# Two conditioning vectors move from TensorE to VectorE rows, a third one's rows move behind the second norm, and the norms get bf16 fillers

## The chip, the core and the metric

The kernel runs on one core of one Trainium2 chip. The metric is the device time of one execution in microseconds (us), as the median of several runs. A core has a matrix engine (TensorE, in the rows PE, with its weight loads as PEld), a vector engine (VectorE, DVE), an engine for functions of one operand (ScalarE, ACT), GpSimd (POOL), SyncE (SP), whose queue issues the DMAs of this kernel, and 16 DMA engines.

## What is computed

Two layers of a decoder trunk on 256 tokens of 1024 channels, all in fp32. In each layer a token mixer (two attentions and a gated 31-tap convolution, weighted by three sigmoid gates) and a channel mixer (up to 2 x 2816 channels, a 3-tap causal convolution, silu(a) * b, down again) are added to `x`. Both are fed by an RMS norm that is scaled and shifted by vectors computed from the condition `c`, and both are multiplied by a gate vector before they are added:

```python
for l in range(2):
    mod = silu(c) @ w_mod[l] + b_mod[l]                      # 6 x 1024 numbers
    sh1, sc1, g1, sh2, sc2, g2 = split(mod, 6)               # parts 0..5
    h = rms_norm(x, mix_norm_g[l]) * (1 + sc1) + sh1
    x = x + g1 * token_mixer(h, ...)
    h = rms_norm(x, ffn_norm_g[l]) * (1 + sc2) + sh2
    x = x + g2 * channel_mixer(h, ...)
```

`(l, r)` is part `r` of layer `l` in what follows: (0,5) is g2 of layer 0, (1,3) is sh2 of layer 1, (1,2) is g1 of layer 1, (1,4) is sc2 of layer 1.

## The kernel before

**Tiles.** `x` lies transposed: 8 tiles of 128 channels by 256 tokens. Every fp32 product is made of three matmuls on pairs of reduced-precision parts (high by high L316, low by high L317, high by low L319; `flush(whole)` in L310 to L312 keeps the three together). A weight unit (mostly 128x1024, 512 KB) is fetched by SP into one of four `raw` buffers; ScalarE rounds it to `whi` (L232), VectorE subtracts to get `wlo` (L233). `take()` keeps two or three split units ahead of the matmuls. The units come in one fixed list, so every engine's order follows from the program's order and from `tc.issue_after`, which holds an instruction behind another one. Instructions on one engine run strictly in that order.

**The conditioning vectors** are computed in two ways. `mod_part(l, r)` does one on TensorE: 8 loads of 512 KB from `wm`, 32 fp32 matmuls (L424), an ACT copy, two transposes (L432), one VectorE addition (L434). `mod_row(l, r, k)` does an eighth of one on VectorE: a load of 512 KB from `wmr`, one multiply-and-accumulate of 128x1024 (L407) against a row `crow`, one small addition (L408). Eight rows make a vector.

**Where they stand.** (0,5) is a `mod_part` that fills the norm ahead of channel mixer 0: two of its eight steps ahead of the sums, six behind, with the transposes after the second up block. (1,3) is a `mod_part` in the same way in the norm ahead of layer 1. Rows of (1,0) and (1,1) run in channel mixer 0, one per up block. The 8 rows of (1,2) are written one behind each `conv_in(k)` at layer 1's start, but nothing holds them there, and they stand among channel mixer 0's instructions on VectorE. They use four spare buffers (`SPARE`). Rows of (1,4) are spread by tokens `r0` to `r1` over the second half of layer 1's token mixer, whose order is the hand-written list `STEPS[1]`: `G` gates, `O` output projections of the attentions, `LS`/`LB` the norm of the convolution, `OC` its projection, `PR` the last projection. The depthwise convolution on VectorE (L1142) runs from `GLU` (L960) to the mean (L1154) ahead of that norm.

**The norm** (`norm_stats`) is a chain: last matmul, residual into `x` (L1290 or L1462), square on ACT, sums on VectorE (L554) and TensorE (L559), rstd on VectorE and POOL (L536, L537), broadcast by two transposes (L569), then tiles `norm_tile` (L615, ACT, L617). Bf16 matmuls that compute nothing (`warm`, L339, "fillers" here) stand in its gaps: `WARM1 = (4, 7, 3)`. Then layer 1 goes on with `conv_in` (L316 into `psa`, halves `conv_in(0)` to `conv_in(7)`), with `latents(k)` (`KL`) behind it.

## Time and profile before

| what | before |
|---|---|
| median of 3 runs | 898.74 us (898.46 to 899.44) |
| the profiled execution: time, and its span | 905.0 us, 902.9 us |
| busy in the span: PE, DVE, ACT, POOL | 881.3, 807.8, 556.9, 50.7 us |
| norm ahead of channel mixer 0: last matmul before, first after | starts 277.74, 285.35 us |
| norm ahead of layer 1: last matmul before, first after | starts 468.15, 476.19 us |
| mean DMA rate | 222 GB/s |

The profiled execution is one run, 6.3 us longer than the median, with 2.1 us of it outside the span. "Busy" of an engine that has work queued behind its own order says little on whether it sets the end: at each stage one has to look which engine's idle time is zero and who waits for whom. Starts in a row are us from the span's start.

### The profile page before, as it was taken

Reading aid. Unit: us, or ns where it says so; the run is one execution under the profiler, and the core shown is the slowest. Engines: PE = TensorE matmul, PEld = TensorE weight load, DVE = VectorE, ACT = ScalarE, POOL = GpSimd, SP = SyncE. Lnnn points to the kernel's source line nnn. Section 1 sums busy time; section 2 is a strip of 40 time slices with the busy share of each in tenths; the row PEclk is TensorE's granted clock in tenths of the full one; section 3 lists DMA queues with packets and bytes.
Section 4 is the critical chain, followed back from the end, with each engine's and each line's share of the span. In section 5 each row is a group of like instructions: output and inputs, shape, how many; then the busy total and the mean of one; then the engine's idle time right before and its main releaser. Section 6 shows DMA issues by size and latency. Waiting matters only on the chain.

```text
span 902.9 us, 18611 instructions
## 1 busy us (share of the span) xinstructions
PE 881.3 (98%) x7247; PEld 836.2 (93%) x7247; DVE 807.8 (89%) x1592; ACT 556.9 (62%) x998; POOL 50.7 (6%) x36
## 2 busy tenths in 40 slices
PE   8999899999999999999999999999999999999998
PEld 6888788998997999999999988989999999999998
DVE  6989899999988999999875999999987899998774
ACT  4677579744666655556543676788465777556551
POOL 1010710000000000000000034000000000000000
PEclk8999999999999999999999999999999999999999
DMA  8956615598998989997752656157866575987631
GB/s 320 376 202 198 196 59 176 183 318 304 318 315 283 332 273 326 301 318 236 214 176 76 202 184 209 53 164 232 264 205 211 163 232 176 308 281 211 194 95 48
DMA packets 57976, 201.59 MB, mean 223 GB/s; under 512 B 6944, under 2 KB 8480, under 8 KB 57888
## 3 DMA queue, kind: packets, MB, share of 16 engines
q1 hardware_dynamic: 57888, 200.41, 66.9%
q8 instruction: 57, 0.93, 0.4%
q14 instruction: 31, 0.25, 0.1%
HBM read 199.33 MB, written 1.05 MB: 222 GB/s over the span
## 4 chain that ended last, share of the span: by engine, by line
PE 76%; DVE 13%; ACT 4%; DMA 4%; issue 2%; SPq 0%; POOL 0%; DVEq 0%; ACTq 0%; POOLq 0%
PE psb L316 15%; PE psb L317 15%; PE psb L319 15%; PE psa L316 7%; PE psa L317 7%; PE psa L319 7%; DVE wlo L233 4%; DVE cacc L1142 2%; ACT whi L232 2%; DVE raw L817 1%; PE psa L424 1%; PE psa L735 1%; PE psa L747 1%; PE psa L680 1%; DMA raw<-in_win 1%
## 5 line engine op out<-in xcount | busy, mean ns | idle before, releaser
L232 ACT ACTIVATE whi<-raw 128x1024 fp32r<-128x1024 f32 (+2 forms) x286 | 295.4, 1041 | 173.7 <-PE psb L317 90.7
L233 DVE TENSOR_TENSOR wlo<-raw,whi 128x1024 fp32r<-128x1024 f32 (+2 forms) x286 | 340.0, 1194 | 48.2 <-ACT whi L232 40.5
L316 PE MATMUL psb<-hh,whi 128*128 128x256 f32 x1056 | 254.7, 282 | 0.6 <-ACT p L714 0.3
L317 PE MATMUL psb<-hl,whi 128*128 128x256 f32 x1056 | 252.3, 279 | 0.0
L316 PEld LDWEIGHTS psb<-hh,whi 128*128 128x128 f32 x1056 | 198.6, 188 | 5.5 <-issue 3.3
L317 PEld LDWEIGHTS psb<-hl,whi 128*128 128x128 f32 x1056 | 198.8, 188 | 0.5 <-DVE wlo L233 0.4
L319 PE MATMUL psb<-hh,wlo 128*128 128x256 f32 x1056 | 144.2, 278 | 0.0
L319 PEld LDWEIGHTS psb<-hh,wlo 128*128 128x128 f32 x1056 | 131.0, 188 | 0.8 <-issue 0.8
L1142 DVE SCALAR_TENSOR_TENSOR cacc<-upad,cw,cacc 128x256 f32<-128x256 f32 x240 | 105.9, 479 | 0.4
L316 PE MATMUL psa<-mhl,whi 128*128 128x256 f32 x400 | 93.3, 277 | 0.0
L317 PE MATMUL psa<-mhl,whi 128*128 128x256 f32 x400 | 93.1, 276 | 0.0
L537 POOL TENSOR_TENSOR rs<-rs,mhalf 128x8 f32<-128x8 f32 (+3 forms) x26 | 49.1, 1900 | 674.4 <-DVE rs L536 674.4
L1424 DVE SCALAR_TENSOR_TENSOR e<-psb,fw,e 128x255 f32<-128x255 f32 (+1 forms) x168 | 79.8, 476 | 4.3 <-ACT e L1422 3.7
L316 PEld LDWEIGHTS psa<-mhl,whi 128*128 128x128 f32 x400 | 74.9, 188 | 0.0
L317 PEld LDWEIGHTS psa<-mhl,whi 128*128 128x128 f32 x400 | 74.9, 188 | 0.0
L1422 ACT ACTIVATE e<-psb,fb,fw 128x256 f32<-128x256 f32 x84 | 46.5, 554 | 37.3 <-DVE e L1424 34.7
L407 DVE SCALAR_TENSOR_TENSOR raw<-raw,crow 128x1024 f32<-128x1024 f32 x56 | 68.1, 1215 | 0.0
L319 PE MATMUL psa<-mhl,wlo 128*128 128x256 f32 x400 | 53.5, 276 | 0.0
L319 PEld LDWEIGHTS psa<-mhl,wlo 128*128 128x128 f32 x400 | 49.1, 188 | 0.0
L1432 ACT ACTIVATE mhl<-e 128x256 fp32r<-128x256 f32 x44 | 18.4, 417 | 43.6 <-DVE e L1430 42.1
L316 PE MATMUL psb<-whi,hh 128*128 128x416 f32 (+1 forms) x96 | 30.8, 349 | 3.2 <-ACT hh L893 3.1
L317 PE MATMUL psb<-whi,hl 128*128 128x416 f32 (+1 forms) x96 | 29.6, 343 | 0.2 <-DVE hl L894 0.2
(295 smaller groups left out, 1522.9 us busy)
## 6 DMA issues: line engine op xcount, KB each, us to landing
raw<-in_wup SPq DMA_DIRECT2D x88, 512.0 KB, 4.9
raw<-in_wmr SPq DMA_DIRECT2D x68, 512.0 KB, 5.4
raw<-in_wdn SPq DMA_DIRECT2D x44, 512.0 KB, 4.6
raw<-in_wgab SPq DMA_DIRECT2D x32, 512.0 KB, 4.9
raw<-in_wqkv SPq DMA_DIRECT2D x24, 512.0 KB, 4.8
raw<-in_wm SPq DMA_DIRECT2D x24, 512.0 KB, 4.4
raw<-in_win SPq DMA_DIRECT2D x16, 512.0 KB, 4.5
raw<-in_wgc SPq DMA_DIRECT2D x16, 512.0 KB, 4.1
```

Source lines behind the costliest of these rows:

```text
L232: ac.activation(hi, raw, AF.Copy)
L233: ve.tensor_tensor(lo, raw, hi.bitcast(F32), op=ALU.subtract)
L316: te.matmul(o, p1[0], p1[1], start=start, stop=False)
L317: te.matmul(o, p2[0], p2[1], start=False, stop=False)
L319: last = te.matmul(o, p3[0], p3[1], start=False, stop=stop)
L407: ve.scalar_tensor_tensor(raw, raw, scale, row, op0=ALU.mult, op1=ALU.mult, accum_out=acc)
L424: te.matmul(acc[32 * c:32 * c + 32, 0:S], cact[:, k:k + 1].to_broadcast([P, 32]), raw[:, c * S:(c + 1) * S], start=(k == 0), stop=(k == KD ...
L537: gp.tensor_tensor(r, r, mhalf[:, :n], op=ALU.pow)
L1142: ve.scalar_tensor_tensor(aj, upad[:, j, t:t + S], cw[:, j * 31 + t:j * 31 + t + 1], aj, op0=ALU.mult, op1=ALU.add)
L1422: ac.activation(t, src, AF.Identity, scale=fw[:, 2, c:c + 1], bias=fb[:, c:c + 1])
L1424: ve.scalar_tensor_tensor(t[:, d:S], src[:, 0:S - d], fw[:, 2 - d, c:c + 1], t[:, d:S], op0=ALU.mult, op1=ALU.add)
L1432: ac.activation(mh, th, AF.Copy)
```

## The change

- (0,5) and (1,3) are not computed on TensorE any more. (0,5) becomes 8 rows at the end of channel mixer 0's rows (`rows_left`), four of them behind late down blocks (`ROWS_LATE`). (1,3) becomes 8 rows in layer 1's token mixer, spread from `r2` to `r3` over `OC0` to `OC7`; the (1,4) rows now end ahead of `OC0` (`r1` moved).
- The rows of (1,2) are held behind the last `norm_tile` of layer 1 and written two each behind `conv_in(4)` to `conv_in(7)` (`GATE_ROWS`). With four buffer tags chosen by `(2 * k + r) % 4`, r = 2 uses two of them.
- `norm_stats` has fillers in place of `fill`: `WARM1 = (8, 6, 8, 7)`, the first 8 directly behind the last real matmul (`newest`). One weight unit that was split between the residuals is kept raw (`later`, `split_rest`) and split behind rstd.
- Layer 1's norm tiles are issued three ahead of `conv_in`, and its weight splits are held behind the last tile issued.

```diff
-WARM1 = (4, 7, 3)
+WARM1 = (8, 6, 8, 7)
+ROWS_LATE = {18: 2, 19: 1, 20: 1}
+GATE_ROWS = {4: (0, 1), 5: (2, 3), 6: (4, 5), 7: (6, 7)}
+LATER = 1
...
-    "OC0 G70 OC1 PR0 OC2 OC3 PR1 OC4 OC5 G71 O6 O7 PR2 OC6 PR3 OC7 PR4 r1 PR5 PR6 PR7 "
+    "r1 r2 OC0 G70 OC1 PR0 OC2 OC3 PR1 OC4 OC5 G71 O6 O7 PR2 OC6 PR3 OC7 r3 PR4 PR5 PR6 PR7 "
...
+    if ("r", 2) in o:
+        o = _spread(o, [("R", 3, k) for k in range(KD)], ("r", 2), ("r", 3))
...
+    def split_rest(keep=0):
+        while len(fetched_raws) > keep:
+            raw, lead, ks = fetched_raws.pop(0)
+            ready.append((split(raw, lead), raw.shape[1] // len(ks), ks))
...
-            ready.append((split(wload_unit(src), lead), src.shape[1] // len(ks), ks))
+            fetched_raws.append((wload_unit(src), lead, ks))
+            split_rest(later[0])
...
-    def norm_stats(fill=None):
+    def norm_stats():
 
-        step(fill or iter(()), F1)
-        bank = psb() if sum(WARM1) else None
+        bank = psb()
+        with tc.issue_after(newest[0].ins):
+            warm(bank, WARM1[0])
         st, last = sq_sums([x[:, k, :] for k in range(KD)], bank)
         with tc.issue_after(last.ins):
-            mid = warm(bank, WARM1[1]) if WARM1[1] else last
+            mid = warm(bank, WARM1[2])
+        r = rstd_of(st, NB, 1.0 / D)
+        hold[0] = [squares[0].ins, rst[0].ins]
+        split_rest()
+        hold[0] = None
         with tc.issue_after(mid.ins):
-            bc = bcast_rows(rstd_of(st, NB, 1.0 / D))
-        if WARM1[2]:
-            with tc.issue_after(rows_last[0].ins):
-                last = warm(bank, WARM1[2])
-        if fill:
-            with tc.issue_after(last.ins):
-                step(fill, KD - F1)
+            bc = bcast_rows(r)
+        with tc.issue_after(rows_last[0].ins):
+            warm(bank, WARM1[3])
         return bc
...
-        fill = mod_part(1, 3, ("oal", "obl", "vb", "lh0", "lh1", "lh2")) if l == 1 else None
...
         for k in range(KD):
             if l > 0:
-                norm_tile(k, bc, gs1[:, k:k + 1], sh1[:, k:k + 1], hh, hl)
+                if k + 3 < KD:
+                    tile(k + 3)
+                hold[0] = [i.ins for i in tiles[-1]]
                 conv_in(k)
-                mod_row(crow1[0], l, 2, k, scale=0.5 if CDMA else 1.0)
+                hold[0] = None
+                for n in GATE_ROWS.get(k, ()):
+                    with tc.issue_after(tiles[-1][1].ins):
+                        mod_row(crow1[0], l, 2, n, scale=0.5 if CDMA else 1.0)
                 continue
...
-            fill = mod_part(l, 5)
-            bc = norm_stats(fill)
+            bc = norm_stats()
...
-        rows_left = [(1, r, k) for r in ((5,) if l else range(2)) for k in range(KD)]
+        rows_left = [(n, r, k) for n, r in (((1, 5),) if l else ((1, 0), (1, 1), (0, 5))) for k in range(KD)]
...
+        def row_next():
+            with tc.issue_after(marks[-1][1].ins):
+                mod_row(crow1[0], *rows_left.pop(0), scale=0.5 if CDMA else 1.0)
...
                 down(j)
+                for _ in range(ROWS_LATE.get(j, 0) if not l else 0):
+                    row_next()
```

In the changed file the lines have other numbers: L407 and L408 are L417 and L418, L233 is L237, L316, L317 and L319 are L326, L327 and L329, L339 is L349, L569 is L583, L615 and L617 are L630 and L632, L960 is L985, L1220, L1221 and L1224 are L1245, L1246 and L1249.

Three places show what moves. The first is TensorE in the norm ahead of layer 1, from the broadcast (`psb` with `rs`) to the first matmul of `conv_in`. Before:

```order
L569 MATMUL psb_6182<-ident,rs_6179 128x128 x2
L339 LDWEIGHTS warm_w
L339 MATMUL psb_6138<-warm_w 128x256
L339 LDWEIGHTS warm_w
L339 MATMUL psb_6138<-warm_w 128x256
L339 LDWEIGHTS warm_w
L339 MATMUL psb_6138<-warm_w 128x256
L424 MATMUL psa_6125<-raw_6188,cact 32x256 x4
L424 MATMUL psa_6125<-raw_6194,cact 32x256 x4
L424 MATMUL psa_6125<-raw_6200,cact 32x256 x4
L424 MATMUL psa_6125<-raw_6206,cact 32x256 x4
L424 MATMUL psa_6125<-raw_6212,cact 32x256 x4
```

A sixth row of four L424 and then the first L316 follow. After the change the first matmuls of `conv_in` stand directly behind seven fillers, of which the last three are shown:

```order
L349 LDWEIGHTS warm_w
L349 MATMUL psb_6121<-warm_w 128x256
L349 LDWEIGHTS warm_w
L349 MATMUL psb_6121<-warm_w 128x256
L349 LDWEIGHTS warm_w
L349 MATMUL psb_6121<-warm_w 128x256
L326 MATMUL psa_6192<-hh_6119,whi_6017 128x256
L326 MATMUL psa_6193<-hh_6119,whi_6017 128x256
L326 MATMUL psa_6194<-hh_6119,whi_6017 128x256
L326 MATMUL psa_6195<-hh_6119,whi_6017 128x256
```

So 24 matmuls leave the place between the broadcast and the first product.

The second place is VectorE at the end of `conv_in` of layer 1, where `upad` is the gated input of the convolution. Before, only weight splits stand ahead of it:

```order
L233 TENSOR_TENSOR wlo_6432<-raw_6429,whi_6431 128x672
L233 TENSOR_TENSOR wlo_6471<-raw_6468,whi_6470 128x672
L233 TENSOR_TENSOR wlo_6510<-raw_6507,whi_6509 128x672
L233 TENSOR_TENSOR wlo_6576<-raw_6573,whi_6575 128x672
L434 TENSOR_TENSOR mod_101<-psa_6544,modb 128x8
L960 SCALAR_TENSOR_TENSOR upad_6551<-e_1096_6558,psa_6226 128x256
```

After:

```order
L237 TENSOR_TENSOR wlo_6431<-raw_6428,whi_6430 128x672
L418 TENSOR_TENSOR mod_101<-m_1066_6425,modb 128x1
L417 SCALAR_TENSOR_TENSOR raw_6458,m_1071_6460<-raw_6458,crow_2273 128x1024
L237 TENSOR_TENSOR wlo_6471<-raw_6468,whi_6470 128x672
L418 TENSOR_TENSOR mod_101<-m_1071_6460,modb 128x1
L417 SCALAR_TENSOR_TENSOR raw_6463,m_1073_6465<-raw_6463,crow_2273 128x1024
L985 SCALAR_TENSOR_TENSOR upad_6511<-e_1090_6518,psa_6192 128x256
```

Six of the eight (1,2) rows now stand ahead of the first L985, two behind the four of them, together with the split of a unit (`wlo_6576` before, `wlo_6536` after) that stood ahead of it before.

The third place is VectorE at the first product of the last projection in layer 1, `PR0`, whose operand is `mhl`. Before:

```order
L233 TENSOR_TENSOR wlo_8730<-raw_8727,whi_8729 128x1024
L1220 SCALAR_TENSOR_TENSOR e_1488_8746<-thc_7397,e_1488_8746 128x256
L1221 TENSOR_TENSOR e_1488_8746<-e_1488_8746,mq_8151 128x256
L1224 TENSOR_TENSOR mhl_8750<-e_1488_8746,mhl_8750 128x256
L233 TENSOR_TENSOR wlo_8757<-raw_8754,whi_8756 128x1024
```

After:

```order
L237 TENSOR_TENSOR wlo_8715<-raw_8712,whi_8714 128x1024
L1245 SCALAR_TENSOR_TENSOR e_1492_8731<-thc_7357,e_1492_8731 128x256
L418 TENSOR_TENSOR mod_101<-m_1533_8942,modb 128x1
L417 SCALAR_TENSOR_TENSOR raw_8885,m_1542_8999<-raw_8885,crow_8177 128x1024
L1246 TENSOR_TENSOR e_1492_8731<-e_1492_8731,mq_8111 128x256
L418 TENSOR_TENSOR mod_101<-m_1542_8999,modb 128x1
L417 SCALAR_TENSOR_TENSOR raw_8940,m_1552_9070<-raw_8940,crow_8177 128x1024
L1249 TENSOR_TENSOR mhl_8735<-e_1492_8731,mhl_8735 128x256
```

Two rows stand between the steps that make the first `mhl`. From the convolution's mean (L1154, now L1179) to this `mhl` there are 6 rows before and 13 after, with 13 weight splits both times.

45 lines of the change are left out of this document (28 added, 17 removed).

## The prediction

> **What bounds the kernel now.** I read the busy times first, then the table of stages, then the rows at the two norms, then VectorE's idle times and the chain of waits. The page's busy times leave two candidates:
>
> ```profile
> PE 881.3 (98%) x7247; PEld 836.2 (93%) x7247; DVE 807.8 (89%) x1592; ACT 556.9 (62%) x998; POOL 50.7 (6%) x36
> ```
>
> The table of stages (PE, PEld, DVE, ACT, POOL busy with counts, clock, DMA share, GB/s) tells which holds where:
>
> ```profile
> 340.00:380.00 40.00, 40.00 (x353) 40.00 (x352) 40.00 (x77) 22.31 (x33) 0.00 (x0) 1.00 0.93 317
> 476.00:499.00 23.00, 23.00 (x205) 22.81 (x198) 10.25 (x17) 9.20 (x16) 0.00 (x0) 1.00 0.31 88
> 499.00:515.00 16.00, 16.00 (x103) 15.66 (x102) 15.91 (x32) 8.64 (x15) 0.00 (x0) 1.00 0.64 199
> 515.00:560.00 45.00, 45.00 (x214) 37.92 (x213) 44.95 (x99) 32.42 (x55) 16.52 (x9) 1.00 0.59 200
> 560.00:610.00 50.00, 49.28 (x427) 45.35 (x426) 49.79 (x108) 41.43 (x110) 2.69 (x2) 1.00 0.36 117
> 610.00:635.00 25.00, 24.85 (x228) 23.82 (x224) 24.83 (x45) 19.00 (x41) 0.00 (x0) 1.00 0.74 234
> 616.00:676.00 60.00, 59.50 (x524) 58.62 (x524) 55.15 (x100) 37.78 (x62) 0.80 (x1) 1.00 0.76 241
> 635.00:674.00 39.00, 38.65 (x336) 38.63 (x337) 34.90 (x66) 23.06 (x37) 0.80 (x1) 1.00 0.74 234
> 660.00:700.00 40.00, 40.00 (x355) 40.00 (x354) 32.72 (x56) 26.37 (x44) 0.00 (x0) 1.00 0.65 205
> ```
>
> Channel mixer 0 (300 to 462) is bound by TensorE: 353 matmuls in 40 us, 0.113 us each. `conv_in` of layer 1 (476 to 499) is too, and VectorE is idle there for 12.75 of 23 us. From 499 to 635 VectorE has 0.52 us idle in 136 us, so each us of VectorE work put in there moves everything on VectorE behind it. From 635 on TensorE sets the end again, and VectorE has room.
>
> **What goes out: the norm of channel mixer 0.** TensorE, then VectorE:
>
> ```profile
> 277.74 0.28 PE L312 MATMUL psa<-mhl,wlo 128*128 128x256 f32 x1
> 282.80 0.43 PE L569 MATMUL psb<-ident,rs 128*128 128x128 f32 x2 [0.31 <-POOL rs L537]
> 283.06 0.49 PE L339 MATMUL psb<-warm_w 128*128 128x256 bf16 x3
> 283.49 1.93 PE L424 MATMUL psa<-raw,cact 128*32 128x256 f32 x32
> 285.35 0.38 PE L316 MATMUL psb<-hh,whi 128*128 128x256 f32 x1
> 287.77 0.64 PE L424 MATMUL psa<-raw,cact 128*32 128x256 f32 x8
> 289.56 0.64 PE L424 MATMUL psa<-raw,cact 128*32 128x256 f32 x8
> ```
>
> ```profile
> 278.46 1.22 DVE L233 TENSOR_TENSOR wlo<-raw,whi 128x1024 fp32r<-128x1024 f32 x1
> 279.59 0.48 DVE L1290 SCALAR_TENSOR_TENSOR x<-psa,g1h,x 128x256 f32<-128x256 f32 x1
> 281.73 0.16 DVE L536 TENSOR_SCALAR rs<-psb 128x2 f32<-128x2 f32 x1 [0.70 <-PE psb L559]
> 283.26 1.26 DVE L615 SCALAR_TENSOR_TENSOR e<-x,gs,psb 128x256 f32<-128x256 f32 x3 [1.37 <-PE psb L569]
> ```
>
> The split at 278.46 takes 1.13 us ahead of the last residual; the change puts it into the 1.37 us in which VectorE waits for the broadcast. The chain does not gain all of it, because sums and fillers on TensorE fill part: I take 0.46 us, so the first tile starts at 282.8. The 32 L424 behind the broadcast (1.86 us from start to next start) go and four more fillers come (7 for 3, 0.11 us apart, as 283.06 to 283.49 shows for the three with their tail), so the first product follows the first `hh`, about 0.9 us earlier than 285.35. The two pieces of eight L424 inside the products go too, 0.45 us net each (their 0.64 less what the next matmul overlaps), with two transposes, 0.25 us. With the 0.46 already in the 0.9 that is 0.9 + 0.9 + 0.25 = 2.05; the four first up units then no longer have their splits late (the L617 at the pace of the tiles), and I take **2.5 us**, from 2.0 to 2.9. It stays, since the next 160 us are TensorE's. VectorE is full there too (40.00 of 40), but carries 24 rows before and after: 8 of (0,5) come, 8 of (1,2) go. The rows cost
>
> ```profile
> L407 DVE SCALAR_TENSOR_TENSOR raw<-raw,crow x56: 1193/1216/1224, 187.2 to 807.4; 128x1024 f32<-128x1024 f32 x56
> ```
>
> 1.22 us, 1.14 from start to next start. Eight `wm` loads leave SP's queue and eight `wmr` of the same 512 KB come later in it: nothing on balance, hidden under a DMA share of 0.93, whose lack of room I leave to the range.
>
> **The norm ahead of layer 1.** Last matmul, the fillings, first product:
>
> ```profile
> 468.15 0.28 PE L312 MATMUL psa<-mhl,wlo 128*128 128x256 f32 x1
> 473.46 2.80 PE L424 MATMUL psa<-raw,cact 128*32 128x256 f32 x48
> 476.19 0.38 PE L316 MATMUL psa<-hh,whi 128*128 128x256 f32 x1
> ```
>
> Up to the broadcast the 16 L424 (1.0 us) give way to 8 fillers and 2 more between sums, so rstd stays where it is. Behind it 2.73 us of L424 go; tiles and 7 fillers let the first product start at 474.3 to 474.9. With the two transposes of (1,3) at the end `conv_in` ends 2.0 us earlier (1.7 to 2.4).
>
> **What that gain meets.** The (1,2) rows now run on VectorE within `conv_in`, where it idles:
>
> ```profile
> 495.92 0.86 DVE L233 TENSOR_TENSOR wlo<-raw,whi 128x672 fp32r<-128x672 f32 x1 [1.51 <-PE psa L319]
> 498.64 0.86 DVE L233 TENSOR_TENSOR wlo<-raw,whi 128x672 fp32r<-128x672 f32 x1 [1.86 <-PE psa L319]
> 499.49 0.74 DVE L960 SCALAR_TENSOR_TENSOR upad<-e,psa 128x256 f32<-128x256 f32 x2
> ```
>
> Six rows stand ahead of L985, and only two buffers serve all eight, so each row waits for the load that follows the row two before it. Rows 0 and 1 are loaded early and run behind the last tile: eight tiles of 0.8 us and five splits of 1.14 from 472.8 on are 485 or a little more, and two rows end at about 487.7. Then a link is a load plus 1.2 us. The chain of waits has two single loads of a row's size, and stages have medians:
>
> ```profile
> 284.18 3.54 DMA raw<-in_wm
> 623.64 3.57 DMA raw<-in_wmr
> ...
> raw<-in_wmr SPq DMA_DIRECT2D x5, 512.0 KB, 4.3
> ...
> raw<-in_win SPq DMA_DIRECT2D x8, 336.0 KB, 2.9
> ```
>
> (4.3 is the median in 616 to 640, 2.9 that of the smaller loads of `conv_in`.) At 3.6 us row 5, two links on, ends at 497.3 and L985 starts when `conv_in` lets it, about 497.4 (0.9 behind its end, as 499.49 was); at 4.4 it starts at 498.9. I take 3.6, since `conv_in` has a DMA share of 0.31. Behind the first L985 VectorE then has two rows (2.4), one split of 672 (0.78) and small additions (0.2) more, and one later row less (1.2): 2.2 us in the stretch that has no room. So the mean of the convolution comes at 497.4 - 499.5 + 2.2 = **0.1 to 0.2 us later** than it would without this norm's change: its gain is eaten. The range is 0 to 2.7 (loads of 4.4: 1.5 at L985, and 1.0 more if rows 6 and 7 are waited for as well).
>
> **The tail of layer 1's token mixer.** The mean, and the first operand of `PR0` with its product:
>
> ```profile
> 635.35 0.67 PE L1155 MATMUL psb<-e,mean_w 128*128 128x256 f32 x2 [0.50 <-DVE mod L408]
> ...
> 673.51 0.43 DVE L1224 TENSOR_TENSOR mhl<-e,mhl 128x256 fp32r<-128x256 f32 x1 [0.48 <-ACT mhl L1223]
> ...
> 674.96 0.28 PE L316 MATMUL psa<-mhl,whi 128*128 128x256 f32 x1
> ```
>
> Between the two VectorE is busy for 34.90 of 39 us and has 1.0 us to spare at `PR0`. Seven more rows stand there (13 for 6): 7 x (1.14 + 0.07) = 8.5 us into 4.1 + 1.0. Not all that was idle can be used, since some waits are for ScalarE; two of TensorE's own waits move as well (its matmuls behind the mean stand 7 nearer to it, 0.8 us). The excess is 8.5 - 5.1 = 3.4 at most; adding up VectorE's row by row at pitch (13 rows 14.8, 13 splits 14.8, the rest 12.4, 42.0 us from the mean to `mhl`, against TensorE's 39.8) gives 2.2. I take **2.6 us**, nearest to the two counts, and the range 0 (VectorE is idle for 7.3 us in 660 to 700 without a wait of TensorE, so lateness may cost nothing) to 3.4. The loads of nine more rows fall into 616 to 676, 14.5 MB before (241 GB/s), 19.2 after: 320 GB/s, just what 340 to 380 shows as possible (317 at a share of 0.93); should they come late, up to 3 us more.
>
> [...]
>
> **The sum.** -2.5 (first norm) + 0.2 (second norm with its rows) + 2.6 (tail) = +0.3 us, on the profiled run's 905.0; on the median of 898.74 that is 899.0. A measurement of this kernel can tell about 0.2%, 1.8 us, from no change.
>
> **Rivals.**
> (a) Gains arrive: the rows at the tail fit (VectorE's 7.3 us of idle time in 660 to 700 absorb them, weights being ahead) and the links take 3.6 us. Then -2.5 + 0.2 + 0 to 0.8, about -2, and with the second norm's end also 0.5 earlier (first product at 474.3), -2.8: 896.2. For it: TensorE idles 0.35 us in 635 to 674, so nothing there is short of VectorE now. Against it: the 13 rows in line.
> (b) Slower: the two-buffer chain. Links of 4.4 us, as in the busier stages, hold L985 until 498.9, and the two late rows and `latents` behind it; +1.5 to +2.7 on the sum, with the tail's 3.4 and some late loads: 901.5. It decides from a load of 4.1 us on, where the mean comes 1 us later.
> (c) The clock. The norms lose their L424, and the granted clock may fall where TensorE waits more, as it does in the first slice:
>
> ```profile
> PEclk8999999999999999999999999999999999999999
> ```
>
> 10 us at 0.8 behind each norm would cost 2 us twice, 903. Against it: the table's stages behind both norms stand at 1.00, and fillers still stand in every gap (waits of 0.3 us at L569). [...]
>
> **Chances.** No change within 0.2% holds 0.37, (a) 0.34, (b) 0.26, (c) 0.03, which is slower with (b). The predicted time is the sum's, 899.0; its own range is 897.0 to 901.0. The range that leaves out two in ten goes from 895.2 (both norms' gains of 4.5 less 1) to 902.4 (b with late loads): faster 0.34, same 0.37, slower 0.29.
>
> **What would show it.** Right: first up matmul 0.9 us nearer to the last projection matmul (7.6 now), and the fourth up unit 2.5; first `conv_in` product 6.1 to 6.8 us behind the last down matmul (8.0 now), no L407-like row waiting more than 1 us in `conv_in`; VectorE with no idle time between L985 and L1179; TensorE waiting for `mhl` or `ul` by 2 to 3 us between L1180 and `PR0`. Wrong: a wait of VectorE for row loads of over 2 us in `conv_in` (then b), no wait of TensorE at `OC0` and `PR0` (then a), a clock under 0.95 in a norm (then c), or a longer channel mixer 0, which would mean that the 24 rows there stand worse than before.

## The result, and the profile after

The changed kernel takes **910.1 us** (median of 6 runs, 908.5 to 911.6) where the kernel before takes 899.35 us (898.5 to 901.5) beside it: ratio **1.0117 [1.0099, 1.0134]**, 10.5 us slower. The forecast was 899.0, with a range to 902.4. A ratio is not always the quotient of two medians.

The profiled execution took 911.43 us, span 909.3 us. Its first lines:

```profile
PE 878.5 (97%) x7145; PEld 838.5 (92%) x7145; DVE 826.1 (91%) x1638; ACT 557.0 (61%) x996; POOL 52.0 (6%) x36
```

TensorE has less to do than before (7145 matmuls for 7247), VectorE has 18.3 us more, and the kernel is longer: the time is in waits. To find the place I compare, stage by stage, the distance between two starts on TensorE, because the start of a stage depends on the run: in the profiled run of before, TensorE's granted clock is 0.83 in the first 20 us and again in 100 to 120 (3.4 us lost in each), which may be most of the distance between its 905.0 us and the median.

| stage, from start to start on TensorE | before, us | after, us | change |
|---|---|---|---|
| last projection product of layer 0 to first up product | 7.61 | 6.91 | -0.70 |
| to the last down product (channel mixer 0) | 182.80 | 183.13 | +0.33 |
| to the first `conv_in` product (second norm) | 8.04 | 6.92 | -1.12 |
| to the first product of `latents` (`conv_in`) | 22.33 | 22.38 | +0.05 |
| to the first product of `UQ` | 21.68 | 26.37 | **+4.69** |
| to the convolution's mean (the attentions) | 115.15 | 120.43 | **+5.28** |
| to the first product of `PR0` | 39.61 | 41.77 | +2.16 |
| to the last projection product of layer 1 | 37.97 | 39.70 | +1.73 |
| to the last down product | 185.71 | 185.07 | -0.64 |

The changes add up to 11.8 us in these two executions, for 10.5 by the ratio. Both norms give something and ten us go in the two stages behind `conv_in`, where VectorE had no room. The same table of stages as in the prediction (columns as there), with windows moved to the same places in the program:

```profile
469.00:492.00 23.00, 22.65 (x195) 22.53 (x195) 18.88 (x35) 11.50 (x19) 0.00 (x0) 1.00 0.60 188
492.00:508.00 16.00, 16.00 (x102) 15.60 (x101) 15.13 (x31) 6.96 (x11) 0.00 (x0) 1.00 0.77 254
508.00:553.00 45.00, 42.45 (x191) 35.19 (x190) 43.53 (x96) 32.29 (x57) 12.14 (x7) 0.96 0.59 195
553.00:603.00 50.00, 48.57 (x396) 44.52 (x394) 50.00 (x107) 35.30 (x86) 10.29 (x4) 1.00 0.35 116
603.00:638.00 35.00, 31.95 (x271) 30.12 (x272) 31.43 (x61) 26.78 (x66) 0.00 (x0) 0.90 0.57 184
638.00:680.00 42.00, 41.03 (x352) 40.64 (x351) 41.62 (x82) 24.63 (x37) 0.80 (x1) 1.00 0.92 324
```

In `conv_in` VectorE now works 18.88 of 23 us (10.25 before) and the DMA share is 0.60 (0.31). Behind it VectorE is *less* busy than before (43.53 of 45, 31.43 of 35) and TensorE too, and the clock is 0.96 and 0.90 where it was 1.00. Two engines that wait for each other look like that. (The wait of 4.4 us "for `p`" is one for room: the next gate products need one of the three `psb` banks, and ScalarE's exponential still has to read scores out of it.) The waits from the second norm to the mean, TensorE's first, then VectorE's from `upad` on (engine, line, what was waited for: us, times, longest):

```profile
PE psb L326 <- ACT p L729: 4.4, 1, 4.4
PE psb L972 <- DVE qll L975: 2.4, 1, 2.4
```

```profile
DVE mx L707 <- PE psa L698: 2.4, 1, 2.4
DVE wlo L237 <- ACT whi L236: 1.8, 3, 0.9
DVE ri L734 <- ACT p L729: 0.8, 1, 0.8
DVE raw L417 <- DMA raw<-in_wmr: 0.5, 1, 0.5
```

Before, TensorE's longest wait in that stretch was 0.5 us, and VectorE had none behind `upad`. How it begins stands on VectorE in `conv_in`. First the first product of `conv_in`, then that of `latents`, which says when `conv_in` has ended on TensorE, then VectorE's rows:

```profile
469.37 0.74 PE L326 MATMUL psa<-hh,whi 128*128 128x256 f32 x4 [0.35 <-ACT hh L631]
...
491.75 0.35 PE L326 MATMUL psb<-whi,hh 128*128 128x416 f32 x1
...
480.08 1.22 DVE L417 SCALAR_TENSOR_TENSOR raw<-raw,crow 128x1024 f32<-128x1024 f32 x1
...
485.58 1.23 DVE L417 SCALAR_TENSOR_TENSOR raw<-raw,crow 128x1024 f32<-128x1024 f32 x1 [0.88 <-DMA raw<-in_wmr]
...
487.50 1.23 DVE L417 SCALAR_TENSOR_TENSOR raw<-raw,crow 128x1024 f32<-128x1024 f32 x1 [0.49 <-DMA raw<-in_wmr]
...
491.39 1.23 DVE L417 SCALAR_TENSOR_TENSOR raw<-raw,crow 128x1024 f32<-128x1024 f32 x1 [1.81 <-DMA raw<-in_wmr]
...
494.52 0.42 DVE L985 SCALAR_TENSOR_TENSOR upad<-e,psa 128x256 f32<-128x256 f32 x1
...
496.55 1.23 DVE L417 SCALAR_TENSOR_TENSOR raw<-raw,crow 128x1024 f32<-128x1024 f32 x1 [0.55 <-DMA raw<-in_wmr]
...
499.39 1.23 DVE L417 SCALAR_TENSOR_TENSOR raw<-raw,crow 128x1024 f32<-128x1024 f32 x1
```

and on SP's queue, where the load of a row can be issued only once the row two before it has been used:

```profile
486.84 0.33 SPq L209 DMA_DIRECT2D raw<-in_wmr  x1
488.76 0.33 SPq L209 DMA_DIRECT2D raw<-in_wmr  x1
```

The fifth row's load is issued at 486.84, when the third row has ended, and the row starts at 491.39: 4.55 us for a load that two single loads before showed at 3.54 and 3.57 (the six loads of this chain that are issued from 481 on took 3.9 to 5.0 us, 4.4 in the median). So `upad` starts 2.77 us behind the first product of `latents` (494.52 - 491.75), where it started 0.97 us behind it before (499.49 - 498.52): 1.80 us late. From `upad` to the mean VectorE was busy 135.3 of 135.9 us before and is busy 138.1 of 144.0 now: 2.8 us more work and 5.4 us more idle time. 1.80 + 2.8 + 5.4 = 10.0, the two bold rows of the table. The first product of `latents` before, and the sums over that stretch, before and after:

```profile
498.52 0.43 PE L316 MATMUL psb<-whi,hh 128*128 128x416 f32 x1
...
sum 135.86, PE 134.64 PEld 122.30 DVE 135.33 ACT 101.36 POOL 19.21; mean PE 33.66 PEld 30.58 DVE 33.83 ACT 25.34 POOL 4.80
```

```profile
sum 144.03, PE 136.76 PEld 123.08 DVE 138.12 ACT 99.98 POOL 22.44; mean PE 34.19 PEld 30.77 DVE 34.53 ACT 25.00 POOL 5.61
```

### The profile page after: what moved, and what is told of

It reads as the page before. It is cut to its first block, busy times and chain, and to the rows that moved or that the text cites. A ratio compares the mean times of both kernels' runs of the same rounds, so it can differ in the third digit from the quotient of the medians.

```text
span 909.3 us, 18428 instructions
## 1 busy us (share of the span) xinstructions
PE 878.5 (97%) x7145; PEld 838.5 (92%) x7145; DVE 826.1 (91%) x1638; ACT 557.0 (61%) x996; POOL 52.0 (6%) x36
## 3 DMA queue, kind: packets, MB, share of 16 engines
HBM read 199.33 MB, written 1.05 MB: 220 GB/s over the span
## 4 chain that ended last, share of the span: by engine, by line
PE 79%; DVE 10%; DMA 5%; ACT 3%; issue 2%; POOL 0%; SPq 0%; DVEq 0%; ACTq 0%; POOLq 0%
PE psb L326 16%; PE psb L327 15%; PE psb L329 15%; PE psa L329 8%; PE psa L327 8%; PE psa L326 7%; DVE wlo L237 3%; DVE raw L831 1%; PE psa L750 1%; PE psa L762 1%; ACT whi L236 1%; DVE raw L417 1%; PE psa L695 1%; ACT p L729 1%; PE psa L320 1%
## 5 line engine op out<-in xcount | busy, mean ns | idle before, releaser
L237 DVE TENSOR_TENSOR wlo<-raw,whi 128x1024 fp32r<-128x1024 f32 (+2 forms) x286 | 340.8, 1197 | 32.8 <-ACT whi L236 32.2
L326 PE MATMUL psb<-hh,whi 128*128 128x256 f32 x1056 | 256.1, 283 | 5.0 <-ACT p L729 4.4
L327 PE MATMUL psb<-hl,whi 128*128 128x256 f32 x1056 | 253.3, 280 | 0.1
L326 PEld LDWEIGHTS psb<-hh,whi 128*128 128x128 f32 x1056 | 199.7, 189 | 9.6 <-ACT p L729 5.0
L327 PEld LDWEIGHTS psb<-hl,whi 128*128 128x128 f32 x1056 | 199.6, 189 | 0.4 <-DVE hl L632 0.3
L329 PE MATMUL psb<-hh,wlo 128*128 128x256 f32 x1056 | 144.7, 278 | 0.0
L329 PEld LDWEIGHTS psb<-hh,wlo 128*128 128x128 f32 x1056 | 131.4, 188 | 0.2 <-issue 0.2
L326 PE MATMUL psa<-mhl,whi 128*128 128x256 f32 x400 | 94.0, 278 | 1.0 <-ACT mhl L1462 1.0
L327 PE MATMUL psa<-mhl,whi 128*128 128x256 f32 x400 | 93.8, 278 | 0.1
L417 DVE SCALAR_TENSOR_TENSOR raw<-raw,crow 128x1024 f32<-128x1024 f32 x72 | 87.8, 1222 | 4.4 <-DMA raw<-in_wmr 4.2
L326 PEld LDWEIGHTS psa<-mhl,whi 128*128 128x128 f32 x400 | 74.9, 188 | 1.3 <-ACT mhl L1462 1.2
L327 PEld LDWEIGHTS psa<-mhl,whi 128*128 128x128 f32 x400 | 74.8, 188 | 0.7 <-DVE mhl L1249 0.4
L329 PE MATMUL psa<-mhl,wlo 128*128 128x256 f32 x400 | 53.9, 277 | 0.0
L329 PEld LDWEIGHTS psa<-mhl,wlo 128*128 128x128 f32 x400 | 49.4, 188 | 0.0
L326 PE MATMUL psb<-whi,hh 128*128 128x416 f32 (+1 forms) x96 | 30.8, 349 | 5.0 <-ACT hh L919 5.0
L326 PE MATMUL psa<-hh,whi 128*128 128x256 f32 x128 | 29.5, 279 | 0.4 <-ACT hh L631 0.4
```

The source lines that it names most:

```text
L237: ve.tensor_tensor(lo, raw, hi.bitcast(F32), op=ALU.subtract)
L326: te.matmul(o, p1[0], p1[1], start=start, stop=False)
L327: te.matmul(o, p2[0], p2[1], start=False, stop=False)
L329: last = te.matmul(o, p3[0], p3[1], start=False, stop=stop)
L417: ve.scalar_tensor_tensor(raw, raw, scale, row, op0=ALU.mult, op1=ALU.mult, accum_out=acc)
```

## The experiments

The rows of the table are changes against before, in us, from the one profiled execution of each; the ratio is against the kernel before on the same chip. "UQ" is the stage from `latents` to `UQ`, "mean" the stage from `UQ` to the mean, and so on as above; the last stage of the first table is left out. One execution can differ from its kernel's median: the profiled ones of "late VectorE work" and "four buffers" are the longest of their twelve (909.16 for a median of 903.80, 909.63 for 904.17), and that of "first norm alone" is 2.6 us above its median. A matmul that only moves from one side of the mean to the other shifts 0.11 us from one column to the next (0.8 us in the changed kernel's own order).

| run | ratio | norm 0 | mixer 0 | norm 1 | conv_in | UQ | mean | PR0 | last product |
|---|---|---|---|---|---|---|---|---|---|
| changed kernel | 1.0117 [1.0099, 1.0134] | -0.70 | +0.33 | -1.12 | +0.05 | +4.69 | +5.28 | +2.16 | +1.73 |
| tanh late | 1.0094 [1.0063, 1.0124] | -0.69 | +0.43 | -1.12 | +0.05 | +3.98 | +5.72 | +1.11 | +1.83 |
| gate rows free | 1.0095 [1.0064, 1.0126] | -0.69 | +6.46 | -1.12 | +0.05 | -0.17 | +0.16 | +4.49 | +0.28 |
| (1,3) on TensorE | 1.0071 [1.0049, 1.0093] | -0.69 | -0.65 | -0.82 | +3.13 | +2.13 | +0.73 | +0.83 | 0.00 |
| before, gate rows held | 0.9995 [0.9977, 1.0014] | 0 | +0.21 | 0 | 0 | +0.02 | +0.71 | 0 | 0 |
| before, late VectorE work | 1.0025 [1.0005, 1.0046] | 0 | +0.21 | 0 | +0.09 | +1.12 | +2.52 | +0.84 | 0 |
| no (1,3) rows | 1.0061 [1.0037, 1.0085] | -0.70 | +0.15 | -1.12 | +0.04 | +4.28 | +6.24 | +0.84 | 0.00 |
| norms alone | 1.0062 [1.0042, 1.0083] | +1.00 | -0.31 | -2.06 | +0.90 | +0.06 | +1.57 | +1.74 | 0 |
| rows early and late | 1.0090 [1.0061, 1.0118] | -0.62 | +0.08 | -1.95 | +0.04 | +3.70 | +0.83 | +1.74 | +1.64 |
| **four buffers** | 1.0009 [0.9987, 1.0031] | -0.69 | -0.06 | -1.12 | +0.12 | +1.15 | +2.63 | +1.54 | +0.25 |
| G11 ahead | 1.0083 [1.0053, 1.0112] | -0.69 | -0.36 | -1.12 | +0.06 | +3.74 | +4.18 | +2.03 | +1.99 |
| four buffers, old loop, G11 | 0.9993 [0.9973, 1.0013] | -0.69 | -0.46 | -1.12 | +1.05 | +0.54 | -0.48 | +1.72 | +1.72 |
| **first norm alone** | 0.9972 [0.9953, 0.9990] | -0.69 | -0.04 | 0 | 0 | +0.04 | +2.45 | +1.54 | 0 |
| four buffers, old loop, G11, no (1,3) rows | 0.9985 [0.9969, 1.0001] | -0.69 | -0.68 | -1.13 | +1.03 | +0.51 | -0.48 | +0.60 | 0 |
| (1,3) in the attentions | 1.0065 [1.0041, 1.0088] | -0.63 | -0.48 | -1.96 | +0.03 | -0.18 | +7.22 | +2.69 | 0 |

**First theories: the tanh, or the late rows.** After the change a tanh of 1.06 us (L1290, for the tail's rows) stands on ScalarE right ahead of the softmax whose `p` TensorE waits for by 4.4 us. The theory was that it is the cause; the rival was VectorE's lateness. The first run holds the tanh back, the second lets the (1,2) rows go where they stood before (the tanh then stands late too).

```diff
-                ac.activation(th, crow1[0], AF.Tanh, scale=0.5)
+                with tc.issue_after(softs[-2][-1].ins) if l == 1 else ExitStack():
+                    ac.activation(th, crow1[0], AF.Tanh, scale=0.5)
```

> The changed kernel, with the tanh of crow in layer 1 (L1290) held behind the first group's last pT copy on ScalarE, where it stood before the change; nothing else. Theory A (the tanh in front of the softmaxes, waiting for its load, costs 4.4 us of TensorE idle time and about 1 us of half clock behind it): 910.1 - 5 = 905, no wait of TensorE for p at 600, clock 1.00 in 600 to 612. Theory B (VectorE is late there anyhow through the rows that were moved, so the tanh only takes the blame): within 1.5 us of 910. Theory C (a fixed cost of the later rows' loads): 908 to 910.

```diff
-GATE_ROWS = {4: (0, 1), 5: (2, 3), 6: (4, 5), 7: (6, 7)}
+GATE_ROWS = {k: (k,) for k in range(8)}
...
-                    with tc.issue_after(tiles[-1][1].ins):
-                        mod_row(crow1[0], l, 2, n, scale=0.5 if CDMA else 1.0)
+                    mod_row(crow1[0], l, 2, n, scale=0.5 if CDMA else 1.0)
```

> The changed kernel, with the (1,2) rows not held behind the last norm tile, one per conv_in(k) as before; they go back to channel mixer 0 on VectorE (32 rows there), and the tanh then stands behind the first softmax group without being held. Theory A with the latents' stall (2.4 us idle at the wait for qll, then half clock: about 4.9 us, caused by the rows' 2.2 us on a full VectorE) : both stalls go, 910.1 - 5 - 4.5 = 900 to 901, unless the 8 rows cost in channel mixer 0, up to 8 x 1.14 = 9 us if VectorE sets its pace there (909). Theory B (tail and loads cost the 10 us): 906 to 910.

With the tanh late little is won: the wait shrinks from 4.4 to 2.7 us, and the stage up to the mean is as long (+5.72). The tanh falls as the cause of the ten us, though the intervals leave it about 2 us; with the tanh held back, ScalarE waits 4.02 us at that place for what VectorE makes of the scores' maximum. With the rows free the 10 us are gone (-0.17, +0.16), so **the rows' place is the cause** of those ten. The kernel as a whole gets hardly faster, because VectorE carries 32 rows in channel mixer 0 then: that stage is 6.1 us longer than in the changed kernel, and the one to `PR0` 2.3. TensorE's wait in that run, for the last operands of channel mixer 0:

```profile
460.87 0.39 PE L320 MATMUL psa<-mhl,whi 128*128 128x256 f32 x1 [3.67 <-ACT mhl L1461]
```

**Does holding the rows cost something by itself?** Here the kernel before with its (1,2) rows held by the change's two lines and nothing else (in its loop that means behind the tile just written, not behind the last one); and the changed kernel with (1,3) as a `mod_part` on TensorE again.

```diff
-                mod_row(crow1[0], l, 2, k, scale=0.5 if CDMA else 1.0)
+                for n in GATE_ROWS.get(k, ()):
+                    with tc.issue_after(tiles[-1][1].ins):
+                        mod_row(crow1[0], l, 2, n, scale=0.5 if CDMA else 1.0)
```

> The kernel before, with only the (1,2) rows held and placed as in the change (two each behind conv_in(4) to conv_in(7)). The tanh stands late as before. Channel mixer 0 has 16 rows for 24. Theory A (the rows on VectorE at conv_in's end push qll back, TensorE waits and its clock halves): +1 to +5, 900 to 904, with a wait for qll. Theory B (VectorE's idle time in conv_in hides the rows): 899 or less, down to 897 if fewer rows help channel mixer 0.

```diff
-            bc = norm_stats()
+            fill = mod_part(1, 3, ("oal", "obl", "vb", "lh0", "lh1", "lh2"))
+            bc = norm_stats(fill)     # two of its steps ahead of the sums, six behind three fillers
...
-    "r1 r2 OC0 G70 OC1 PR0 ... OC7 r3 PR4 PR5 PR6 PR7 "
+    "OC0 G70 OC1 PR0 ... OC7 PR4 r1 PR5 PR6 PR7 "
```

> The changed kernel, with (1,3) computed on TensorE again as filler of the norm ahead of layer 1, and the (1,4) rows spread as before; the held (1,2) rows stay. Theory A (the held rows and the order of the tanh are the cost; it stands early here too): about 910 - 4 (tail) + 1.3 (norm) = 907 to 908, the waits for p and qll still there. Theory B (the eight (1,3) rows at the tail cost most): 901 to 903.

Held rows cost the kernel before nothing (0.9995): all eight get ahead of `upad`, and `upad` stands 0.97 us behind `latents`, as without them. The buffers are not the difference, since the rule that gives these rows two of the four spare buffers is in the kernel before as well, and the loads take 4.5 us in the median there, for 4.4 after the change. The chain of eight rows is 18.6 us long there from first start to last, and 19.3 after the change. What differs is where it starts: 1.39 us behind the first product of `conv_in`, for 10.71 in the changed kernel (480.08 - 469.37), where all rows are held behind the last of eight tiles and four splits stand among these tiles.

```profile
470.28 0.38 PE L317 MATMUL psa<-hh,whi 128*128 128x256 f32 x1
...
471.67 1.22 DVE L408 SCALAR_TENSOR_TENSOR raw<-raw,crow 128x1024 f32<-128x1024 f32 x1
```

So it is a two-buffer chain of 19 us that starts too late for a `conv_in` of 22 us. With (1,3) on TensorE the 2.8 us of matmuls stand within `conv_in` (+3.13), all eight rows get ahead of `upad`, which starts 4.00 us behind `latents`, and the loss behind `conv_in` is 2.9 us, not 10: there 3.0 us of lateness at `upad` pass one to one.

**How much is lateness alone?** The kernel before with held rows and two more VectorE instructions of a row's shape behind the last `upad`, and the changed kernel without the eight (1,3) rows (the part is its bias alone, so the products of sh2 are left out).

```diff
+            if l == 1 and j == 3:
+                for _ in range(2):
+                    junk = wk.tile([P, D], F32, tag="oah", ...)
+                    with tc.issue_after(up.ins):
+                        ve.scalar_tensor_tensor(junk, crow1[0], 1.0, crow1[0], op0=ALU.mult, op1=ALU.mult, accum_out=small(1, "m0", 4))
```

> The kernel before, with its (1,2) rows held among conv_in's instructions as in the run before_gate_rows_held (which took 0.9995 of before's time), and two more VectorE instructions of a row's shape (1.2 us each) behind the last upad, whose results nobody uses. Nothing of the norms, of (0,5), (1,3) or of the tail is changed. VectorE has no room between there and the mean of the convolution. If lateness of VectorE passes one to one, as my prediction had it: +2.4 us, 902, and no wait of TensorE over 1.5 us. If it grows (TensorE runs out of operands for some us, its clock is halved behind that, and the order in the attentions is laid out anew): +4 to +8 us, 904 to 908, with at least one wait of TensorE over 2 us for qll or a softmax's p and a clock of 0.5 behind it; the start of the mean moves by 4 us or more. If VectorE could take the work in after all: 900.

```diff
-    "r1 r2 OC0 G70 OC1 PR0 ... OC7 r3 PR4 PR5 PR6 PR7 "
+    "OC0 G70 OC1 PR0 ... OC7 PR4 r1 PR5 PR6 PR7 "
...
+            ve.tensor_copy(mod[1][:, 24:32], modb[:, 1, 24:32])
```

> The changed kernel without the eight rows of (1,3) (the part is taken as its bias alone, so 8 loads, 8 multiplications and 8 additions are left out) and with the (1,4) rows spread as before. Everything up to the mean of the convolution is as in the changed kernel, in the same order. If the tail costs what the ledger says (2.2 us from the mean to PR0 and 1.7 from PR0 to the last projection product): 906.2, with the two stretches back at 39.6 and 38.0 us, and the +10 us up to the mean unchanged. If the tail's lateness is only what the attentions left behind: 909.5 to 910 and both stretches as long as after the change.

2.4 us of late work cost 0.25% (2.3 us, 0.5 to 4.1): about one to one by the ratio, with one wait of 2.35 us for `p`. (Its profiled execution, the longest of twelve, shows 3.6 us in the two stages, of which 2.2 are idle time of VectorE.) So one late piece is not multiplied much; what the change has is twice that, 4.6 us. Without the (1,3) rows the ratio falls by 0.6%, and in the table the tail falls by 2.16 + 1.73 - 0.84 = 3.05 us.

**The norms alone, and the rows elsewhere.** Two tries to keep the gains. The first is the kernel before and was meant to get only the norms' part (with (1,3) as its bias alone); the second is the changed kernel with before's loop, meant to put the (1,2) rows ahead of `upad`, and with the (1,3) rows behind the operands of the last projection.

```diff
-            bc = norm_stats(fill)
+            bc = norm_new()            # the fillers alone, at both norms
+GATE_ROWS = {k: (k,) for k in range(8)}
```

> The kernel before with (0,5) as rows in channel mixer 0, the new norm with its fillers at both places, the (1,2) rows held one behind each conv_in, and nothing kept raw. The rows of (1,3) are left out (its bias alone is taken), and the tail is before's. So the norms' part stands alone, without the two late gate rows behind upad and without the tail's rows. If the norms' gains are real and stay where VectorE isn't late: first up matmul 0.7 us nearer, conv_in's first product 1.1 us nearer, at most 0.5 given back in channel mixer 0 and 0.6 at the attentions: 897.5 to 898.5 where before takes 899.5. If a gain of TensorE there only turns into a wait for VectorE at qll and a softmax: 899.5 to 902, with a wait of TensorE of over 1.5 us between 510 and 610 us.

```diff
-LATER = 1
+LATER = 0
...
-    "r1 r2 OC0 G70 OC1 PR0 OC2 ... OC7 r3 PR4 PR5 PR6 PR7 "
+    "OC0 G70 OC1 PR0 r2 OC2 ... OC7 PR4 r1 PR5 PR6 r3 PR7 "
...
+            with tc.issue_after(out_last[0].ins) if r == 3 and l == 1 and out_last[0] else ExitStack():
                 use_row(fetched[used[0]], crow1[0], l, r, k, 0.5 if CDMA else 1.0)
```

> The changed kernel in which all eight (1,2) rows run ahead of upad (conv_in's tiles and products in before's order, no split kept raw for it), and the (1,3) rows are held, each behind the newest operand of the last projection, PR0 to PR7, where VectorE was idle for 11 of 51 us before. It computes all that the reference does. If the change's costs are the lateness of VectorE behind upad and the rows ahead of PR0, both are gone and the norms' gains of 1.8 us stay, less 0.5: 897.5 to 899, with the mean no later than before and 37 to 38.5 us from PR0 to the last projection product. If rows in the last projection delay its operands all the same, or their loads come late: 900 to 902, with that stretch at 39.5 us or more.

Both missed. In the first, rows that nothing held there had moved into layer 0's tail and its norm (an L409 at 266.09 ahead of an operand that TensorE waits 1.94 us for), so it says nothing on the first norm. In the second the rows still use two buffers, and their chain starts 5.0 us behind the first product of `conv_in` and is 19.5 us long: `upad` starts 4.22 us behind `latents`, TensorE waits 2.8 us for `qll`, and all of the 1.95 us that the second norm gave is lost there. And with most of the rows in the last projection VectorE is left with 1.2 us of idle time in its 39.6: the last (1,3) row is late for channel mixer 1.

```profile
516.79 0.44 PE L966 MATMUL psb<-ident,ma 128*128 128x128 f32 x2 [2.83 <-DVE qll L969]
...
720.26 0.80 PE L326 MATMUL psa<-u,whi 128*128 128x258 f32 x2 [3.93 <-ACT u L657]
```

**Four buffers.** If the chain of loads makes the rows late, the cure is one line: the (1,2) rows take all four spare buffers in turn. The rival, that the halved clock behind the waits (0.50 in 516 to 518 and in 604 to 610 us of the changed kernel's span) makes a good part of the loss, is tried by giving TensorE other work at the longer wait.

```diff
-        return wload(wmr[ROWS.index((l, r)), k], *(tag or (SPARE[(2 * k + r) % 4], 1)))
+        return wload(wmr[ROWS.index((l, r)), k], *(tag or (SPARE[k % 4 if (l, r) == (1, 2) else (2 * k + r) % 4], 1)))
```

> The changed kernel with one difference: the (1,2) rows take all four spare buffers in turn, where the change's rule gives them two. All eight rows then stand ahead of upad, and the order in the attentions is nearly before's. If the lateness of VectorE there (1.8 us at upad and 2.8 us of work behind it) is the cause of the loss between conv_in and the mean: upad 1.0 to 1.5 us behind the first product of latents (2.8 after the change, 1.0 before), waits of TensorE for qll and p under 2 us each, the mean 6 to 9 us earlier, 901.5 to 904; the tail's 3 us stay. If the loads are late all the same, with a DMA share of 0.9 between 480 and 495, or the order of the attentions was never decisive: 907 to 910.

```diff
-    "BA12 C30 G11 C31 BA13 ..."
+    "BA12 G11 C30 C31 BA13 ..."
```

> The changed kernel with two neighbours in the hand-written list exchanged: G11 ahead of C30, so that TensorE has 4.5 us of products in an open bank where it waits 4.4 us for p after the change. VectorE's work, its rows and its order up to there are as after the change. If a part of the loss is made by the halved clock behind that wait (VectorE then idles 2.4 us for TensorE's scores): clock 1.00 from 600 to 612, no wait of TensorE over 1.5 us there, the mean 2.5 to 5 us earlier, 905.5 to 907.5. If VectorE alone sets the end of this stretch and the halved clock only fills time that is lost anyway: 909 to 910.5, and the wait stands at C30 or later.

The one line takes 1.0117 to **1.0009 [0.9987, 1.0031]**. The chain is 12.4 us long instead of 19.3, all eight rows now stand ahead of `upad`, the order of the attentions is nearly before's, and TensorE's waits are down to 1.2 us for `qll` and 0.4 us for `p`. The first product of `latents`, the last row and `upad` in that run:

```profile
496.66 0.35 PE L326 MATMUL psb<-whi,hh 128*128 128x416 f32 x1
...
497.39 1.23 DVE L417 SCALAR_TENSOR_TENSOR raw<-raw,crow 128x1024 f32<-128x1024 f32 x1 [0.36 <-DMA raw<-in_wmr]
...
498.54 0.42 DVE L985 SCALAR_TENSOR_TENSOR upad<-e,psa 128x256 f32<-128x256 f32 x1
```

1.88 us after `latents`, not the 1.0 to 1.5 of the expectation. **The two-buffer chain is the cause**: one line takes the loss back. The +2.63 at the mean is mostly one wait of that execution for a row of (1,4). The runs "first norm alone" and "before, gate rows held" have it too (2.43 and 0.75 us), and their ratios are 0.9972 and 0.9995, so it needn't show in the median; whether held (1,2) rows make it likelier is not shown. The wait:

```profile
628.76 1.23 DVE L417 SCALAR_TENSOR_TENSOR raw<-raw,crow 128x1024 f32<-128x1024 f32 x1 [2.15 <-DMA raw<-in_wmr]
```

G11 ahead has a ratio in the range expected of it (1.0083, an interval that still meets the changed kernel's), but not by what was to bring it: TensorE waits 4.16 us for `p` one step earlier in its list, and the clock behind it is 0.77, 0.50 and 0.88 in the three windows of 2 us from 604 to 610. The order of those two was not the cause.

**What became of the norms' gains.** With VectorE on time, the rest of the change can be weighed: all of it with four buffers, G11 ahead of C30 and before's loop; then only the first norm's part (with the (1,2) rows held, one behind each `conv_in`, as (0,5) takes their place in channel mixer 0); then the first of these without the (1,3) rows (their part is its bias alone); then both norms with (1,3) spread over the attentions on TensorE, with four buffers, before's loop and tail, and the (1,2) rows one behind each `conv_in`.

```diff
-            for k in range(3):
-                tile(k)
...
+                tile(k)
                 conv_in(k)
```

> Both of these together, and conv_in's tiles and products in before's order (which brings its first product 0.9 us nearer than the change's). It computes all that the reference does. If VectorE on time lets the norms' gains arrive: -0.4 (first norm, with what channel mixer 0 gives back) and -2.0 (second), +3.0 for the 13 rows of the tail: 900.1, with the mean 1 to 2 us earlier than before by the same start. If TensorE's gain at the second norm only turns into a wait for qll again (TensorE 2 us earlier, VectorE not): 902 to 904, with a wait of 1.5 us or more at qll.

```diff
+            fill = mod_part(1, 3, ("oal", "obl", "vb", "lh0", "lh1", "lh2"))
+            bc = norm_old(fill)        # before's norm ahead of layer 1, its loop, its tail
+GATE_ROWS = {k: (k,) for k in range(8)}
```

> Of the change only what concerns the norm of channel mixer 0: (0,5) as rows at the end of channel mixer 0's rows, the fillers there, the one split kept raw; the (1,2) rows are held, one behind each conv_in. The norm ahead of layer 1, (1,3) on TensorE, conv_in's loop and the tail are before's, and so is the order of the attentions. If the first norm's gain is the 0.7 us of the ledger, less 0 to 0.3 given back in channel mixer 0: 898.8 to 899.2 where before takes 899.5. If the first down block's wait for its operand or late loads eat it, or VectorE's stretch behind conv_in sets the end: 899.5 to 900.5. By my prediction's step it should be 897.0.

```diff
+            ve.tensor_copy(mod[1][:, 24:32], modb[:, 1, 24:32])     # in place of the (1,3) rows
```

> The run four_buffers_old_loop_gate_ahead (0.9993 of before's time) without the eight (1,3) rows in the tail: the part is its bias alone, so 8 loads, 8 multiplications and 8 additions are left out, and the (1,4) rows are spread as before. The order up to the mean is the same. If both norms' gains arrive once VectorE is on time, and the tail's rows take them back: from the mean to the last projection product 3.0 to 3.4 us less, 0.9955 to 0.9965 of before's time. If the tail's rows cost only what the attentions leave behind, or the norms' gains end as VectorE's waits: 0.998 to 1.000.

```diff
-LATER = 1
+LATER = 0
-PARTS = [[(0, r) for r in (2, 3, 4) if (0, r) not in RPARTS], []]
+PARTS = [[(0, r) for r in (2, 3, 4) if (0, r) not in RPARTS], [(1, 3)]]
```

> A version that keeps both norms' part and avoids what the runs showed to cost: the (1,2) rows one behind each conv_in with four buffers, no split kept raw in the norms, conv_in's tiles and products in before's order, the tail as before, and (1,3) as a mod_part whose 32 matmuls are spread over layer 1's attentions (as the kernel does it for a part of layer 0), where VectorE sets the pace and TensorE has room. It computes all that the reference does. If the norms' gains (-0.6 and -1.9 us) arrive when VectorE is on time and the new TensorE work is hidden there: 896.5 to 897.5 where before takes 899.5, ratio 0.9965 to 0.998. If the matmuls or their eight loads delay an attention, or the new order there leaves TensorE a wait of 1.7 us for p again: 899 to 901.

The whole change with four buffers and before's loop is as fast as before (0.9993). Without the tail's (1,3) rows it is 0.9985, less than was expected, though its two tail stages are 2.84 us shorter; the comparison can't tell 0.7 from 2.8 us here. **The first norm alone has the lowest ratio: 0.9972 [0.9953, 0.9990]**, 0.9 to 4.2 us faster than before and, by the two ratios, 1.4% faster than the changed kernel; its interval overlaps that of the whole change with four buffers. Its profiled execution doesn't show the gain: it has 0.7 us in the norm and channel mixer 0, but +2.45 at the mean (the row wait above) and +1.54 at `PR0`.

The run with (1,3) in the attentions shows that the norms' gains can arrive: by the first product of `UQ` it is 3.2 us ahead of before (-0.63 - 0.48 - 1.96 + 0.03 - 0.18), with `upad` on time:

```profile
489.42 0.35 PE L326 MATMUL psb<-whi,hh 128*128 128x416 f32 x1
...
490.45 1.41 DVE L979 SCALAR_TENSOR_TENSOR upad<-e,psa 128x256 f32<-128x256 f32 x4
...
570.18 3.45 PE L695 MATMUL psa<-qkT 96*128 96x256 f32 x8 [2.19 <-ACT p L729]
```

Then the attentions, whose order the 32 matmuls changed, and the stage behind them give back 9.9 us; from `upad` to the mean VectorE idles 7.4 us more than before. (1,3) costs something wherever it is put, in `conv_in` (+3.1), in the attentions (+9.9) or in the tail (+3): the norm's gap, where it stood before, was the cheapest place that was tried (without it that stage is 1.1 to 2.0 us shorter).

## Why the prediction was wrong, step by step

- **First norm, -2.5 predicted.** The first up matmul came 0.70 us nearer, not 0.9. I had put the kept split (1.23 us) at no cost into VectorE's wait for the broadcast, as a gain of 0.46. In the two runs that keep no split raw ("rows early and late" and "(1,3) in the attentions") the product comes 0.62 us nearer, so keeping it gained 0.07. It isn't free there, because GpSimd computes rstd in that wait and takes 1.55 us with the split beside it:

```profile
272.41 0.28 PE L322 MATMUL psa<-mhl,wlo 128*128 128x256 f32 x1
...
275.94 1.23 DVE L237 TENSOR_TENSOR wlo<-raw,whi 128x1024 fp32r<-128x1024 f32 x1
...
276.17 1.55 POOL L547 TENSOR_TENSOR rs<-rs,mhalf 128x2 f32<-128x2 f32 x1 [50.97 <-DVE rs L546]
...
277.78 0.43 PE L583 MATMUL psb<-ident,rs 128*128 128x128 f32 x2 [1.06 <-POOL rs L547]
279.32 0.50 PE L326 MATMUL psb<-hh,whi 128*128 128x256 f32 x2 [0.35 <-ACT hh L631]
```

  Before, the same GpSimd instruction took 0.70 us (next fence). The pieces of L424 and the transposes within the products, 1.6 us by my count, brought TensorE another 1.0 us by the sixth up unit. Then the first down block waits 0.99 us for its operand, which stands on ScalarE behind a rounding whose weights came late, and that 1.0 us is gone. Their load was issued at 289.65 and landed 6.44 us later, where the median of such loads is 4.7 over the span; the DMA share from there to 296.2 is 0.80. I read that as the lack of room that I had left to the range; no run tries it.

```profile
282.04 0.70 POOL L537 TENSOR_TENSOR rs<-rs,mhalf 128x2 f32<-128x2 f32 x1 [50.97 <-DVE rs L536]
```

```profile
296.17 1.06 ACT L236 ACTIVATE whi<-raw 128x1024 fp32r<-128x1024 f32 x1 [2.31 <-DMA raw<-in_wup]
...
297.58 0.38 PE L326 MATMUL psa<-mhl,whi 128*128 128x256 f32 x1 [0.99 <-ACT mhl L1462]
```

  So -0.4 in the stages up to the end of channel mixer 0 (-0.3 to -1.4 in the other runs with this norm, but for the two with more rows on VectorE there), for -2.5: by the stages the mechanism was right and the term too large, the kept split and the pieces within the products above all. The ratio of the run with the first norm alone says otherwise, -2.5 us (0.9 to 4.2), just the forecast; which of the two is right stays open.
- **Second norm, first product 6.1 to 6.8 us behind the last down matmul.** It is 6.92 us, with GpSimd's 1.53 us in it again; in the two runs with the new norm in which no split stands beside it (0.69 us in "rows early and late") it is 6.09 and 6.08, the lower edge of the forecast. `conv_in` ended 1.07 us earlier, not 2.0.
- **"What that gain meets", +0.1 to 0.2 at the mean: this step failed.** Three numbers in it were wrong. The load in the link of the two-buffer chain took 4.4 us in the median (3.9 to 5.0), not 3.6; rival (b) had it at 4.4. I chose 3.6 by the DMA share of 0.31 that `conv_in` had before, but with these loads in it the share was 0.60. The work behind `upad` was 2.8 us for 2.2. And above all I added these up as if VectorE would be busy without a break, that is, I put its idle time at nothing: from `upad` to the mean it came to 5.4 us more than before. Of its waits of 5.5 us there, 3.2 stand at a softmax, where VectorE waits for ScalarE's `p` (0.8) and for TensorE's scores (2.4) while TensorE had waited for ScalarE; 1.8 are for weights that ScalarE rounds, and 0.5 for a row's load. That a late VectorE stops the engines that feed it is a reading of these waits, not an experiment of its own. Lateness alone doesn't bring the idle time: with (1,3) on TensorE `upad` is 3.0 us late and VectorE idles 0.7 us more. I had also looked at three places of the order only. Between the first product of `UQ` and the mean, 30 of VectorE's 234 instructions (rows left out) stand in another order than before, and 15 of 231 with four buffers. That order alone isn't the cause, since in the run with late VectorE work 39 do, and it cost 2.3 us. How the 5.4 us divide between order, lateness and clock stays open.
- **Tail, +2.6 predicted.** 3.05 us in one pair of profiles and 2.84 in another: right in size, half wrong in place. I had all of it ahead of `PR0` and called VectorE's idle time behind it room; of the 3.05 us 1.32 came up to `PR0` and 1.73 behind it.
- **Rivals.** (b), slower by the two-buffer chain, is what happened, decided by the load of over 4.1 us that it named; its price of +1.5 to +2.7 was about a quarter of what it came to, at most. (a) had a chance of 0.34 and rested on links of 3.6 us (its 896.2 is a slip too: 898.74 - 2.8 is 895.9). (c), the clock, was given 0.03. It fell, not in the norms (1.00 in 272 to 279 and in 462 to 469) but behind the two waits (0.50 in 516 to 518 and in 604 to 610).

## What to carry to other kernels

Before work is moved into an engine's idle time, follow its loads: as many buffers as the work is deep decide whether idle time is usable, and here one line (four buffers for two) was worth 1.1%. Ask also when the first of these loads can start: the same chain of 19 us was harmless 1.4 us into its stage and late at 10.7. In a stretch in which one engine sets the pace and others feed it, lateness of that engine needn't pass as a sum: 4.6 us became 10 here, while 3.0 us stayed 2.9 in another run. A gap that looks wasted may be the cheapest place for the work that fills it.
